# A decoder layer in fp32 on one core: the heads' scratch tiles of even and odd heads from one pool of fourteen slots instead of two of seven

## The chip, the core and the metric

The kernel runs on one core of a Trainium2 chip. The metric is the device time of one execution in microseconds, taken on the chip; lower is better. The core has a matrix engine (TensorE, PE in the profile), three engines for elementwise work (VectorE or DVE, ScalarE or ACT, GpSimd or POOL), and SyncE (SP), which in this kernel issues nearly all transfers between DRAM and the on-chip memory. Each engine runs its own instruction stream in order and waits on semaphores for the others.

## What is computed

One layer over 2048 tokens of width 1024, in fp32: a gated DeltaNet mixer with eight heads and a four-head attention over 256 memory rows, both read from one input projection; one output projection of the concatenated heads; a layer norm; a squared-ReLU MLP of width 4096; a layer norm.

```python
def gdn_mixer(x, mem_k, mem_v, w_in, conv_w, a_log, dt_bias, gate_norm_w, w_out):
    proj = x @ w_in                         # q, k, v, z, a, b, mq
    qkv = silu(causal_depthwise_conv(qkv, conv_w))
    q, k = l2_normalize(heads(q)), l2_normalize(heads(k))
    beta = sigmoid(b); g = -exp(a_log) * softplus(a + dt_bias)
    o = chunk_gated_delta_rule(q, k, v, g, beta)
    o = rms_norm(o, gate_norm_w) * silu(heads(z))
    m = memory_attention(mq, mem_k, mem_v)
    return concat([o, m]) @ w_out
...
x = layer_norm(ALPHA * x + mix)
x = layer_norm(ALPHA * x + square(relu(x @ w1)) @ w2)
```

In the delta rule each chunk of tokens inverts a unit lower triangular matrix (1 + beta k k^T with decay, below the diagonal) and then updates a state of 128 x 128 per head, chunk after chunk.

## The kernel before

**Blocks and stages.** The tokens go in four blocks of 512 (TB). For each pair of blocks (the loop over s at line 1752) come: the mixer of block 2s, the mixer of block 2s+1, the output projection of both (out_seven), the MLP's first product (ff1) and its second (ff2). A block's tokens are handled in chunks of 128, four at a time in one tile (NC). The projections and the MLP run as three fp32r products each (a high and a low part of both operands, mm3 at line 547). The output projection and the MLP use a scheme of seven products instead of eight for two blocks of tokens by two halves of the weights, so they keep sums of operands (S1 to S4, T1 to T4) in DRAM.

**The mixer.** The function mixer (line 1582) steps t from 0 to 9. In each step it records gdn_b for head t-2, then gdn_a for head t-1, then dense for head t, then a gate projection, memory heads and other work.
- dense(h) projects q, k and v, runs the convolution (ACT copies each PSUM bank to one of two raw tiles, DVE adds three taps from it), splits q and k into the tiles kq0 and kq1 (one buffer each), and writes kd, the transposed k with its decay (line 824).
- gdn_a(h) loads gb, a row of decays broadcast to all partitions (line 980), makes dl and at from it with a select on POOL and four exponentials on ACT each (lines 992 to 1003), multiplies both by the product pkq of k with k and q, two chunks at a time in one PSUM bank (lines 1005 to 1013), inverts dl (invert, line 851: an elimination loop of fifteen steps on DVE in the tiles Bc and Xc, then small matmuls through the single-buffered tiles of inv), keeps the inverse in Y, and makes vb and qd.
- gdn_b(h) runs the four chunks of the scan. It is a chain of PE, DVE, PE, ACT, PE, DVE per chunk and reads kd, at, Y, vb and qd to its end. The result goes to deliver (line 1203), which in the odd blocks also forms differences with the block before; for heads 6 and 7 it splits one of them into an "xh" and an "xl" tile at line 1230 for the product S2.

**The slots.** The function slot (line 463) asks for a tile of 128 x 512 fp32 from the pool sp under a tag; the number of slots of each tag is in BUFS (line 460). Seven tiles of a head (kd, gb, dl, at, Y, vb, qd) come from "s0" for even heads and from "s1" for odd heads, seven slots each. gb and dl are last read inside gdn_a, the other five by gdn_b. The same two tags serve later stages: in out_seven the tiles f (line 1679, "s0") and the low halves xl of operands S3, S4 and A22 as loaded from DRAM (line 1639: "s0" for n == 5, otherwise "s1"; six tiles for each of n = 3, 5 and 6); in ff1 operands kept through the stage (second_half, lines 1261 to 1263 and 1295); in ff2 the low halves of the last product (line 1470, alternating).

**The order of the work.** Nothing is issued while the functions above run. They only record operations (Recorder). At the end rec.issue (line 291) replays all of them with a duration for each, engine by engine: at every point the engine that can start first takes, among its operations that are ready, the one recorded first (rec.shift moves a few, rec.gate holds transfers back). A tile takes its slot when the first operation on it is otherwise ready. Slots of a tag are promised in the order in which the tiles are first used in the recording: a tile may take a free slot only if there are more free slots than tiles ahead of it that still have none. The lines that do this:

```python
if len(slots[b.key]) <= ahead(b):
    wait[b.key].append(o)
    return
b.held = True
b.since = heapq.heappop(slots[b.key])
```

The order found is the order in which the instructions stand in every engine's stream, so a changed number of slots can move any instruction behind the first tile that is touched by it. PSUM banks are tags of the same kind: "acc" with three banks for projections, "ga0" and "ga1" for gdn_a of even and odd heads, "pb" with two for gdn_b, "m".

Of the kernel before, what the change touches and what calls it, by code (L numbers as in the profile page):

```python
# [418 lines left out]
def hybrid_layer(  # L419
# [37 lines left out]
    dr = ctx.enter_context(tc.tile_pool(name="dr", bufs=2, space=bass.MemoryType.DRAM))  # L457

    NW, NR = 4, 3
    BUFS = {"d": 11, "th": 2, "s0": 7, "s1": 7, "on": 1, "iv": 4}  # L460
    PBUFS = {"acc": 3, "ga0": 1, "ga1": 1, "pb": 2, "m": 1}

    def slot(name, tag="s0", dt=F32, shape=(P, TB)):
# [331 lines left out]
    def dense(b, h, T, G, w0=None):  # L795
        res = {}
        for nm, o in (("q", QO), ("k", KO), ("v", VO)):
            w = w0 if w0 and nm == "q" else load_in(b, o // P + h)
            a = bank("a" + nm, "acc")
            project(a, w, T)  # L800
            c = slot("c" + nm, "d")
            th = slot("th", "th")
            if True:
                gi = o // P + h
                raw = rec.buf(tp, (P, TB + 3 + 56), F32, "raw", 2, "raw")
                nc.scalar.copy(out=raw[:, 3:TB + 3], in_=a)
                nc.gpsimd.tensor_copy(raw[:, 0:3], halo[:, gi].part(gi))
                if b < NB - 1:
                    nc.gpsimd.tensor_copy(halo[:, gi].part(gi), raw[:, TB:TB + 3])
                nc.scalar.activation(c, a, AF.Copy, scale=cw[:, 72 + gi:73 + gi])  # L810
                for j in range(3):
                    nc.vector.scalar_tensor_tensor(out=c, in0=raw[:, j:j + TB], scalar=cw[:, j * 24 + gi:j * 24 + gi + 1],
                                                   in1=c, op0=ALU.mult, op1=ALU.add)
                nc.scalar.activation(th, c, AF.Tanh, scale=0.5)
                nc.vector.scalar_tensor_tensor(out=c, in0=th, scalar=1.0, in1=c, op0=ALU.add, op1=ALU.mult)
            res[nm] = c
            if nm in "qk":
                if "kq" not in res:
                    res["kq"] = [rec.buf(tp, (P, 2, TB), F32R, "kq%d" % u, 1, "kq") for u in range(2)]
                i = "kq".index(nm)  # L820
                split(c, res["kq"][0][:, i].part(i), res["kq"][1][:, i].part(i), KQE)
        par = "ga%d" % (h % 2)
        ss = small("ss", [P, 2 * NC])
        kd = res["kd"] = slot("kd", "s%d" % (h % 2))
        for n, nm in enumerate("kq"):
            pt = bank("pt" + nm, par)
            for c in range(NC):
                nc.tensor.transpose(pt[:, c * P:(c + 1) * P], res[nm][:, c * P:(c + 1) * P], ident)
            for c in range(NC):
                j = small("j" + nm, [P, P], 1)  # L830
                nc.scalar.activation(j, pt[:, c * P:(c + 1) * P], AF.Square,
                                     accum_out=ss[:, n * NC + c:n * NC + c + 1])
            if nm == "k":
                for c in range(NC):
                    nc.scalar.activation(kd[:, c * P:(c + 1) * P], pt[:, c * P:(c + 1) * P], AF.Copy,
                                         scale=G["ekd"][:, h, c:c + 1])
        nc.gpsimd.tensor_scalar_add(ss, ss, 4 * RMS_EPS)
        rk = small("rk", [P, NC])
        nc.gpsimd.tensor_tensor(out=rk, in0=ss[:, :NC], in1=mhalf, op=ALU.pow)
        res["e4"] = small("e4", [P, NC], 4)  # L840
        nc.gpsimd.tensor_scalar_mul(res["e4"], ss[:, NC:], P * RMS_EPS)
        res["vbs"] = small("vbs", [P, NC])
        nc.gpsimd.tensor_tensor(out=res["vbs"], in0=G["betah"][:, h], in1=rk, op=ALU.mult)
        bh = res["bh"] = small("bh", [P, NC])
        nc.gpsimd.tensor_tensor(out=bh, in0=G["beta"][:, h], in1=rk, op=ALU.mult)
        nc.gpsimd.tensor_tensor(out=bh, in0=bh, in1=rk, op=ALU.mult)
        res["nbe"] = small("nbe", [P, NC], 4)
        nc.gpsimd.tensor_tensor(out=res["nbe"], in0=bh, in1=G["neg"][:, h], op=ALU.mult)
        return res

    def invert(L, par):
# [37 lines left out]
        ZT = small("ZT32", [P, NC, 32], 2)  # L889
        nc.vector.transpose(ZT.rearrange("p c f -> p (c f)"), Z.rearrange("p c f -> p (c f)"))  # L890
        XB, LB, X32, X64, Q = (inv[n] for n in ("XB", "LB", "X32", "X64", "Q"))
        Y = slot("Y", "s%d" % par)
        Y3 = v4(Y)
        nc.gpsimd.memset(Y, 0.0)
        quads = [slice(32 * q, 32 * q + 32) for q in range(4)]
# [79 lines left out]
    def gdn_a(h, r, G):  # L975
        par = h % 2
        q, k, v = (r[n] for n in "qkv")
        q3, k3, v3 = v4(q), v4(k), v4(v)
        sc = lambda n, c: G[n][:, h, c:c + 1]
        gb = slot("gb", "s%d" % par)  # L980
        nc.sync.dma_start(out=gb, in_=G["scr"][4 * h:4 * h + 4].rearrange("c i -> (c i)").partition_broadcast(P))
        gb3 = v4(gb)

        def trans(a3, nm):
            pt = bank(nm, "ga%d" % par)
            for c in range(NC):
                nc.tensor.transpose(pt[:, c * P:(c + 1) * P], a3[:, c], ident)
            return v4(pt)

        kd3 = v4(r["kd"])  # L990
        bh, vbs = r["bh"], r["vbs"]
        dl = slot("dl", "s%d" % par)
        dl3 = v4(dl)
        nc.gpsimd.affine_select(out=dl3, in_=gb3, compare_op=ALU.is_gt, fill=1e30,
                                base=0, pattern=[[0, NC], [-1, P]], channel_multiplier=1)
        for c in range(NC):
            nc.scalar.activation(dl3[:, c], dl3[:, c], AF.Exp, bias=sc("gc", c), scale=-1.0)
        at = slot("at", "s%d" % par)
        at3 = v4(at)
        nc.gpsimd.affine_select(out=at3, in_=gb3, compare_op=ALU.is_ge, fill=-1e30,  # L1000
                                base=0, pattern=[[0, NC], [1, P]], channel_multiplier=-1)
        for c in range(NC):
            nc.scalar.activation(at3[:, c], at3[:, c], AF.Exp, bias=sc("ngc", c))
        kh, kl = r["kq"]
        for c0 in range(0, NC, 2):
            pkq = bank("pkq", "ga%d" % par).rearrange("p (c u f) -> p c u f", c=2, u=2)
            for c in (c0, c0 + 1):
                cs = slice(c * P, (c + 1) * P)
                mm3(pkq[:, c - c0], kh[:, 0, cs], kl[:, 0, cs], kh[:, :, cs], kl[:, :, cs], True, True)
            for c in (c0, c0 + 1):  # L1010
                nc.vector.scalar_tensor_tensor(out=dl3[:, c], in0=pkq[:, c - c0, 0], scalar=bh[:, c:c + 1], in1=dl3[:, c],
                                               op0=ALU.mult, op1=ALU.mult)
            nc.vector.tensor_tensor(out=at3[:, c0:c0 + 2], in0=pkq[:, :, 1], in1=at3[:, c0:c0 + 2], op=ALU.mult)
        Y3 = invert(dl3, par)

        pv = trans(v3, "ptv")
        vb = slot("vb", "s%d" % par)
        vb3 = v4(vb)
        for c in range(NC):
            nc.scalar.activation(vb3[:, c], pv[:, c], AF.Copy, scale=vbs[:, c:c + 1])  # L1020
        qd = slot("qd", "s%d" % par)
        nc.scalar.activation(qd, gb, AF.Exp)
        nc.vector.tensor_tensor(out=qd, in0=qd, in1=q, op=ALU.mult)
        qd3 = v4(qd)

        return dict(k3=k3, kd3=kd3, vb3=vb3, at3=at3, qd3=qd3, Y3=Y3, nbe=r["nbe"], e4=r["e4"])
# [232 lines left out]
    def second_half(ys, T0d, B, between):  # L1259

        homes = {"T3": [slots("d", 4), slots("s0", 4)], "T2": [slots("d", 3), slots("s0", 3), halves("kq0", 1)],
                 "T4": [slots("s1", 3), slots("th", 2), slots("on", 1), halves("kq1", 1)],
                 "T1": [halves("tok", 4)], "B22": [slots("s1", 4), slots("iv", 4)]}
        homes = {n: [p for g in h for p in g] for n, h in homes.items()}
        for n, h in homes.items():
            B[n] = h[:4], h[4:]
# [25 lines left out]
                split(t3, B["T3"][0][k][:, c], B["T3"][1][k][:, c])  # L1292
        between()
        for k in K2:
            t4[k] = slot("b21", "s1")
            nc.sync.dma_start(out=t4[k], in_=T0d[:, 4 + k])
            t2 = wide("t2")
            sub(t2, e[k], t1[k])
            place("T2", k, t2)
            sub(t4[k], t4[k], t2)  # L1300
# [124 lines left out]
    def ff2(s, x1d):  # L1425
        ys = [tok_tile("y") for _ in range(2 * NC)]
        fresh = [[True, True] for _ in range(2 * NC)]
        gb = []
# [32 lines left out]
        def xpart(n, u, last):  # L1461
# [4 lines left out]
                return [(hi[:, j], lo[:, j]) for j in range(2)]  # L1466
            r = []
            for j in range(2):
                hi, lo = slot("xh", "d", F32R), slot("xl", "s%d" % j, F32R)
                split_in_place(hi, lo, xsc[n][:, 2 * u + j].part(2 * u + j))  # L1470
                r.append((hi, lo))
            return r
# [147 lines left out]
    def out_seven(s, x1d, T0d):  # L1620
# [10 lines left out]
        def operand(n, name, u):  # L1631
            if name == "S2" and u == 1:
                return [Xd[6], Xd[7]]
            if not XH[n][u]:
                x = []
                for j in range(2):
                    k = 2 * u + j
                    hi = slot("xh", "d" if n % 2 or k < 5 else "on", F32R)
                    lo = slot("xl", "s0" if n == 5 else "s1", F32R)
                    split_in_place(hi, lo, xo[name][:, k].part(k))  # L1640
                    x.append((hi, lo))
                return x
# [186 lines left out]
```

## Time and profile before

| | us |
|---|---|
| median of 3 runs | 2760.96 |
| lowest and highest | 2760.94, 2762.19 |
| the profiled execution, its own time | 2760.71 |
| its span, first to last instruction | 2759.0 |

The profile is of one execution. Its page gives each engine's busy time, a table in slices, the chain of work that ended last, and groups of instructions; further views list waits, the instructions of one tile, the order of time, and the busy time of each engine in chosen stretches. Since all operations are issued from one line of the program (402), tiles tell them apart. In a row such as "dl<-pkq,bh,dl" the written tile stands to the left. "[2.64 <-ACT whl]" behind a row means that the engine stood idle for 2.64 us before it and that an ACT instruction writing whl ended the wait, as far as the semaphores tell. PE is the matmul engine, PEld its weight loads, which overlap. PEclk is the granted clock of PE as a share of full speed. "x4" is the number of instructions put together in a row. In time the stages are: mixers of blocks 0 and 1 up to about 640, the first output projection up to about 790, the MLP up to about 1400, and the same again for blocks 2 and 3, with mixers to about 2010.

### The profile page before, as it was taken

What the parts mean: (1) busy time and instruction counts of PE and PEld (TensorE: products, weight loads), DVE (VectorE), ACT (ScalarE), POOL (GpSimd) and SP (SyncE); (2) the same over time, 40 slices, a digit from 0 to 9 for tenths busy, and PEclk for the clock granted to TensorE, in tenths of its full rate; (3) what the DMA queues carried; (4) which work ended last, traced back from release to release, by engine and by line L of the source; (5) the groups of instructions that cost most, each with busy time, mean ns of one, the idle gap of its engine ahead of it and who ended that gap; (6) DMA issues with size and microseconds to landing.
All of it is one profiled execution on the core that took longest, in us unless ns stands there. A gap on an engine that the chain in (4) does not pass through costs nothing.

```text
span 2759.0 us, 42405 instructions
## 1 busy us (share of the span) xinstructions
PE 2719.8 (99%) x13589; PEld 2267.0 (82%) x13589; DVE 2112.2 (77%) x5652; ACT 1642.3 (60%) x4082; POOL 403.7 (15%) x1030
## 2 busy tenths in 40 slices
PE   9999999999999999999999999999999999999998
PEld 7888888887788888888888888888887788888887
DVE  7889889998777777665778887888978665657575
ACT  7678767676485556334446676677855655544342
POOL 3233223321000000000023321223201000000000
PEclk9999999999999999999999999999999999999999
DMA  8565558876788888766754344444578744477673
GB/s 327 207 234 205 215 182 288 290 258 228 269 284 302 280 285 297 268 211 205 265 209 149 138 155 174 169 147 159 206 251 280 249 145 152 163 252 243 205 239 116
DMA packets 208543, 613.99 MB, mean 223 GB/s; under 512 B 23072, under 2 KB 32192, under 8 KB 188352
## 3 DMA queue, kind: packets, MB, share of 16 engines
q1 hardware_dynamic: 207888, 611.23, 63.5%
q8 instruction: 107, 1.75, 0.2%
q14 instruction: 116, 0.95, 0.1%
q10 hardware_dynamic: 432, 0.05, 0.0%
HBM read 436.54 MB, written 174.65 MB: 222 GB/s over the span
## 4 chain that ended last, share of the span: by engine, by line
PE 88%; ACT 7%; DVE 4%; issue 1%; POOL 1%; DMA 0%; DVEq 0%; SPq 0%; POOLq 0%; ACTq 0%
PE f2A L402 13%; PE fA L402 12%; PE ao L402 8%; PE f2C L402 6%; PE fC L402 6%; PE az L402 5%; PE aq L402 5%; PE av L402 5%; PE ak L402 5%; PE f2B L402 3%; PE fB L402 3%; PE amq L402 3%; PE pc L402 3%; PE po L402 2%; PE pkq L402 1%
## 5 line engine op out<-in xcount | busy, mean ns | idle before, releaser
L402 DVE TENSOR_TENSOR whl<-wraw,whl 128x512 fp32r<-128x512 f32 (+2 forms) x294 | 257.2, 884 | 109.4 <-ACT whl L402 107.0
L402 ACT CAST whl<-wraw 128x512 fp32r<-128x512 f32 (+2 forms) x294 | 226.5, 780 | 158.0 <-PE fC L402 52.0
L402 PE MATMUL fA<-B,whl 128*128 128x512 f32 x1152 | 277.2, 389 | 1.8 <-ACT B L402 1.5
L402 ACT CAST X<-X 128x1024 fp32r<-128x1024 f32 x118 | 123.9, 1052 | 236.2 <-DMA X<-xsc 196.2
L402 PE MATMUL f2A<-whl,X 128*128 128x512 f32 x1152 | 262.1, 389 | 0.0
L402 PEld LDWEIGHTS fA<-B,whl 128*128 128x128 f32 x1152 | 216.1, 188 | 47.5 <-ACT B L402 1.9
L402 PEld LDWEIGHTS f2A<-whl,X 128*128 128x128 f32 x1152 | 216.2, 188 | 44.9
L402 DVE TENSOR_TENSOR X<-X,X 128x1024 fp32r<-128x1024 f32 x118 | 144.2, 1223 | 129.0 <-ACT X L402 128.8
L402 PE MATMUL aq<-T,whl 128*128 128x512 f32 x768 | 214.3, 408 | 10.0 <-ACT T L402 5.5
L402 PE MATMUL az<-T,whl 128*128 128x512 f32 x768 | 213.0, 406 | 0.0
L402 PE MATMUL ak<-T,whl 128*128 128x512 f32 x768 | 211.4, 406 | 0.0
L402 PE MATMUL av<-T,whl 128*128 128x512 f32 x768 | 210.4, 404 | 0.0
L402 PE MATMUL fC<-B,whl 128*128 128x512 f32 x768 | 185.4, 389 | 0.3 <-DVE B L402 0.3
L402 PE MATMUL f2C<-whl,X 128*128 128x512 f32 x768 | 174.7, 389 | 0.0
L402 PEld LDWEIGHTS fC<-B,whl 128*128 128x128 f32 x768 | 144.1, 188 | 30.7 <-DVE B L402 0.8
L402 PEld LDWEIGHTS f2C<-whl,X 128*128 128x128 f32 x768 | 144.1, 188 | 29.9
L402 PEld LDWEIGHTS aq<-T,whl 128*128 128x128 f32 x768 | 136.5, 191 | 32.7 <-ACT T L402 5.5
L402 POOL TENSOR_SCALAR ve<-mv 128x1 f32<-128x1 f32 x34 | 16.4, 483 | 962.0 <-DVE mv L402 961.5
L402 PEld LDWEIGHTS av<-T,whl 128*128 128x128 f32 x768 | 137.3, 189 | 22.7
L402 PEld LDWEIGHTS ak<-T,whl 128*128 128x128 f32 x768 | 136.4, 189 | 23.5
L402 PEld LDWEIGHTS az<-T,whl 128*128 128x128 f32 x768 | 135.9, 189 | 21.6
L402 PE MATMUL ao<-whl,X 128*128 128x512 f32 x528 | 140.1, 404 | 3.5 <-DVE whl L402 1.3
(287 smaller groups left out, 6300.8 us busy)
## 6 DMA issues: line engine op xcount, KB each, us to landing
whl<-wsc SPq DMA_DIRECT2D x108, 1024.0 KB, 4.8
wraw<-in_w_ff_dram SPq DMA_DIRECT2D x106, 512.0 KB, 4.5
X<-xsc SPq DMA_DIRECT2D x96, 512.0 KB, 3.9
wsc<-whl SPq DMA_DIRECT2D x36, 1024.0 KB, 5.2
whl<-tsc SPq DMA_DIRECT2D x64, 512.0 KB, 4.7
xsc<-hB SPq DMA_DIRECT2D x96, 256.0 KB, 3.4
xo<-cat SPq DMA_DIRECT2D x80, 256.0 KB, 3.9
wraw<-in_w_in_dram SPq DMA_DIRECT2D x35, 512.0 KB, 5.9
```

The source lines that it names most:

```text
L402: o.fn(*[res(a) for a in o.args], **{k: res(v) for k, v in o.kw.items()})
```

## The change

The tag "s1" goes away and "s0" has fourteen slots. Every tile that came from "s1", or from "s0" or "s1" by the parity of its head, now comes from "s0". Memory, operations and their recorded order stay as they were.

```diff
-    BUFS = {"d": 11, "th": 2, "s0": 7, "s1": 7, "on": 1, "iv": 4}
+    BUFS = {"d": 11, "th": 2, "s0": 14, "on": 1, "iv": 4}
...
-        kd = res["kd"] = slot("kd", "s%d" % (h % 2))
+        kd = res["kd"] = slot("kd", "s0")
...
-        Y = slot("Y", "s%d" % par)
+        Y = slot("Y", "s0")
...
-        gb = slot("gb", "s%d" % par)
+        gb = slot("gb", "s0")
...
-        dl = slot("dl", "s%d" % par)
+        dl = slot("dl", "s0")
...
-        at = slot("at", "s%d" % par)
+        at = slot("at", "s0")
...
-        vb = slot("vb", "s%d" % par)
+        vb = slot("vb", "s0")
...
-        qd = slot("qd", "s%d" % par)
+        qd = slot("qd", "s0")
...
-                 "T4": [slots("s1", 3), slots("th", 2), slots("on", 1), halves("kq1", 1)],
-                 "T1": [halves("tok", 4)], "B22": [slots("s1", 4), slots("iv", 4)]}
+                 "T4": [slots("s0", 3), slots("th", 2), slots("on", 1), halves("kq1", 1)],
+                 "T1": [halves("tok", 4)], "B22": [slots("s0", 4), slots("iv", 4)]}
...
-            t4[k] = slot("b21", "s1")
+            t4[k] = slot("b21", "s0")
...
-                hi, lo = slot("xh", "d", F32R), slot("xl", "s%d" % j, F32R)
+                hi, lo = slot("xh", "d", F32R), slot("xl", "s0", F32R)
...
-                    lo = slot("xl", "s0" if n == 5 else "s1", F32R)
+                    lo = slot("xl", "s0" if n == 5 else "s0", F32R)
```

The PSUM banks "ga0" and "ga1" still go by the parity of the head.

## The prediction

> **What bounds the kernel now.** I read the page first, then the busy time of each engine by stage, then TensorE's waits and the order of time around them.
>
> ```profile
> span 2759.0 us, 42405 instructions
> PE 2719.8 (99%) x13589; PEld 2267.0 (82%) x13589; DVE 2112.2 (77%) x5652; ACT 1642.3 (60%) x4082; POOL 403.7 (15%) x1030
> PE 88%; ACT 7%; DVE 4%; issue 1%; POOL 1%; DMA 0%; DVEq 0%; SPq 0%; POOLq 0%; ACTq 0%
> ```
>
> TensorE (PE) is busy for all but 2759.0 - 2719.8 = 39.2 us, and the chain that ends last runs through it for 88%. The change adds and removes no arithmetic, so it can act only on those 39.2 us and on the clock. The table by stage says where they lie (columns: stretch, its length, then each engine's busy time; PEclk near the end).
>
> ```profile
> core 0: us, PE busy (x) PEld busy (x) DVE busy (x) ACT busy (x) POOL busy (x), PEclk, DMA share, GB/s
> 0.00:69.00 69.00, 62.82 (x288) 49.05 (x289) 53.15 (x108) 51.70 (x125) 25.79 (x64) 1.00 0.90 327
> 138.00:620.00 482.00, 479.07 (x2704) 404.43 (x2703) 430.98 (x1632) 358.73 (x1178) 144.18 (x362) 1.00 0.67 239
> 620.00:640.00 20.00, 17.27 (x98) 13.59 (x96) 18.14 (x72) 17.67 (x51) 6.66 (x13) 1.00 0.78 245
> 640.00:695.00 55.00, 54.17 (x298) 45.79 (x298) 47.45 (x160) 32.62 (x93) 6.77 (x18) 1.00 0.68 239
> 695.00:715.00 20.00, 16.52 (x79) 13.25 (x78) 10.55 (x18) 7.70 (x22) 1.46 (x3) 0.83 0.64 225
> 1448.00:2000.00 552.00, 548.47 (x3117) 465.78 (x3116) 460.93 (x1858) 385.54 (x1319) 144.31 (x412) 1.00 0.46 162
> 2000.00:2207.00 207.00, 203.86 (x980) 167.33 (x979) 155.05 (x311) 121.55 (x238) 11.23 (x26) 1.00 0.76 260
> 2690.00:2759.00 69.00, 59.77 (x264) 49.17 (x262) 39.95 (x54) 14.04 (x17) 6.29 (x8) 0.96 0.33 116
> ```
>
> The first and last slices hold 6.2 + 9.2 = 15.4 us that slots of the heads cannot reach. The mixers proper idle only 2.9 us (138 to 620) and 3.5 us (1448 to 2000). The end of block 1's mixer, 620 to 715, idles 2.7 + 0.8 + 3.5 = 7.0 us; the same place in block 3 lies within the 3.1 us of 2000 to 2207. One more stretch matters, because a gap there also cost clock:
>
> ```profile
> 82.00:84.50 2.50, 0.15 (x2) 0.00 (x0) 2.50 (x12) 1.62 (x4) 0.24 (x1) 1.00 0.00 0
> 84.50:91.30 6.80, 4.65 (x18) 3.97 (x19) 6.80 (x30) 0.35 (x1) 0.45 (x1) 0.50 0.30 93
> 702.00:705.70 3.70, 2.01 (x11) 1.34 (x10) 1.59 (x4) 1.84 (x6) 0.00 (x0) 1.00 0.52 167
> 705.70:712.50 6.80, 5.01 (x14) 3.86 (x15) 3.88 (x6) 4.36 (x13) 1.46 (x3) 0.50 0.48 163
> 2158.00:2166.00 8.00, 6.24 (x27) 4.60 (x26) 8.00 (x15) 5.97 (x12) 0.00 (x0) 1.00 0.92 335
> ```
>
> Twice the granted clock was 0.50 for 6.8 us, each time from inside a gap; 6.8 us at half rate are 3.4 us lost. The gap near 2160 (8.00 - 6.24 = 1.8 us) cost no clock. So the tail of block 1 loses 3.5 us idle and 3.4 us of clock within ten microseconds, and its cause is a slot:
>
> ```profile
> 702.64 0.39 PE L402 MATMUL po<-state,qd 128*128 128x128 f32 x2
> 703.06 1.93 SPq L402 DMA_DIRECT2D xl<-xo  x4
> 707.34 0.62 ACT L402 CAST xh<-xl 128x512 fp32r<-128x512 f32 x1
> 707.49 2.50 PE L402 MATMUL ao<-whl,xh 128*128 128x512 f32 x5 [2.64 <-ACT whl L402]
> ```
>
> The fourth product of the output projection (S3, line 1639) takes its xl tiles from "s1", which head 7 fills. Its last four loads are issued when the final read of head 7's qd ends (703.03), the first cast follows at 707.34, and PE stands for 2.64 us.
>
> **The change, part by part.** A head takes seven slots: kd, gb, dl, at, Y, vb, qd. gb and dl are given back inside gdn_a, the other five by gdn_b. With seven slots per parity, head h+2 gets kd and gb from head h's gb and dl, and everything else must wait for gdn_b of head h. That wait shows in the view of the tile dl and in the order of time for block 1's head 7:
>
> ```profile
> L402 ACT ACTIVATE dl<-dl,gc x128: 385/402/508, 65.1 to 1968.5; 128x128 f32<-128x128 f32 x128
> ...
> L402 POOL TENSOR_SCALAR_AFFINE_SELECT dl<-gb x32: 631/683/1097, 64.0 to 1966.7; 128x512 f32<-128x512 f32 x32
> ...
>   PE po L402: 39.5, 15
> ...
> 577.93 0.38 SPq L402 DMA_DIRECT2D gb<-scr  x1
> 601.67 0.63 ACT L402 ACTIVATE qd<-gb 128x512 f32<-128x512 f32 x1
> 610.37 0.22 DVE L402 COPY inv<-dl 64x128 f32<-64x128 f32 x1
> 622.25 0.76 PE L402 MATMUL pkq<-kq 128*128 128x256 f32 x5
> 624.44 0.39 PE L402 MATMUL po<-state,qd 128*128 128x128 f32 x2
> 624.91 0.68 POOL L402 TENSOR_SCALAR_AFFINE_SELECT dl<-gb 128x512 f32<-128x512 f32 x1 [0.57 <-PE po L402]
> 628.15 0.33 DVE L402 SCALAR_TENSOR_TENSOR dl<-pkq,bh,dl 128x128 f32<-128x128 f32 x1
> 631.84 0.41 DVE L402 TENSOR_TENSOR at<-pkq,at 128x256 f32<-128x256 f32 x1
> 632.31 0.98 PE L402 MATMUL pkq<-kq 128*128 128x256 f32 x6
> ```
>
> The input gb was fetched from 577.93 and the first pkq pair was done at 622.25 + 0.76 = 623.0. Yet dl began at 624.91, as head 5's last qd read (624.44 + 0.39) ended, the products at 628.15, and the second pair, waiting for the PSUM bank, at 632.31. In 15 of 32 heads POOL's idle time before dl ended on such a po.
>
> In one pool of fourteen the places are kept in order of first use: five for head h, five for head h+1 once its gb and dl are back, four for kd, gb, dl, at of head h+2. So dl and at no longer wait for gdn_b(h) but for gb and dl of head h+1. For head 7 those came back at 601.67 + 0.63 = 602.3 and 610.6, and then kq sets the pace: the products could follow the pair at 623.0 instead of at 628.15 and 631.84, 5.1 to 8.8 us sooner. I carry 6.
>
> What this moves: two selects of 0.68 us on POOL, which is 15% busy; eight exponentials on ACT, some 3.2 us at the 0.40 us of a row of this kind; on DVE the six products. All are as many as before. Behind the two selects POOL has the Y memset, which stays with gdn_b(h) and is read late. On SP the gb load falls back in the line: it was issued 47.0 us ahead of dl; it would now take the place that head 6's gb gives back at 602.3, still 22.6 us ahead of 624.91. Behind it on SP stand weight and X loads, issued in planned order. The cost is 0; uncovered it would be a load of this queue, 4.3 us by the xl rows above (703.06 to 707.34). kd of head h+3 now stands behind Y, vb, qd of head h+2, which take places at the same gdn_b end; cost 0.
>
> Two uses get worse places. In the odd blocks line 1230 asks for an xl for head 6's difference ahead of head 7's gb, so one of the fourteen is kept for it until its first write:
>
> ```profile
> L402 DVE TENSOR_TENSOR xl<-cat,xh x2: 685/687/689, 693.9 to 714.9; 128x512 fp32r<-128x512 f32 x2
> ```
>
> It is kept from 610 to 693.9, and head 7's at is the one that misses its place: it must still wait for head 5's gdn_b. And S3's six xl stand behind four f: 14 - 5 - 2 - 4 leaves 3 early loads against 2 now. The last three still wait for gdn_b(7).
>
> The sum. Head 6 is not touched by the kept place, so gdn_b(5) and (6) come 6 us sooner and at of head 7 with them. PE reaches S3 at about 702 either way; the loads need 4.3 us from the release, so a gdn_b(7) that ends 4.5 us sooner closes the gap. Terms: -3.5 us (702 to 707.5), -3.4 us (no half clock), -0.8 us of the 2.7 idle at 620 to 640, where ACT has both sets of exponentials and a memory softmax at once. Against that, the front of each inversion now competes for DVE (431.0 of 482.0 us busy): the 2.9 and 3.5 us of idle in the mixers grow; no row prices this. Bounds: they vanish (-6.4 us) or double (+6.4 us); I take +1.6, a quarter, since DVE's work is the same and only its order changes. Net -6.1 us: 2760.7 us, the profiled execution's own time (1.7 us outside the span), becomes 2754.6; the median shown is 2760.96, so I say 2755.
>
> The clock's price can be read in two ways. The row is 6.8 us at 0.50. The Trainium skill (TensorE: Matmul & The Clock Gate, "Why this matters for your kernels") asks for no idle gap above about 3 us, and gives a busy window of 3.4 us to come back. The trace disagrees with both: a 2.64 us gap went with the half clock and it lasted twice that. By 3.4 us at half rate the term would be -1.7 and the sum 2756.3.
>
> **The rivals.** (1) The tail stays. DVE, not the slot, sets head 7's chain, and the place kept for line 1230 eats the lead. For: DVE was busy 18.1 of 20.0 us at 620 to 640. Against: ACT and the slot, not DVE, delayed the products. Only the 0.8 us goes: 2760.
>
> (2) The change does not do what it says: Y, vb and qd of head h+1 are still without places when head h+2 asks, and the line is as long as two short ones. For: places are kept in order. Against: gb and dl of the head before are back 14 us before dl starts. 2761.
>
> (3) The gap closes but the half clock comes anyway, from the ragged stretch of 702 to 705.7 (2.0 of 3.7 us busy): -3.5 - 0.8 + 1.6, so 2758. The gate rows speak for it as far as 1.8 us near 2160 passed and 2.64 us here did not. The Trainium skill's 3 us (the same section) would have it so, since 2.64 us alone should not have tripped the clock.
>
> (4) Slower. Today head 7's elimination loop starts as head 6's ends; at the start of block 0 heads 0 and 1 ran theirs in step, and PE starved with DVE full.
>
> ```profile
> 82.44 0.25 DVE L402 TENSOR_TENSOR Bc<-Bc,Lc 128x24 f32<-128x24 f32 x2
> ...
> 641.02 0.22 DVE L402 TENSOR_TENSOR Xc<-Xc,Bc 128x60 f32<-128x60 f32 x1
> 641.15 0.16 DVE L402 TENSOR_TENSOR Bc<-Bc,Lc 128x4 f32<-128x4 f32 x1
> ```
>
> With dl sooner the loops overlap, the later head's steps go ahead of the next dense's taps (recorded later), raw's two tiles stay full, and the PSUM banks with them. The price is that of 82 to 91.3: 2.35 + 2.15 idle + 3.4 clock = 7.9 us, once, with the tail as it is: 2769. It decides where DVE has no slack for as long as the banks last. Against: DVE has a tenth of its time left in the mixers.
>
> **How the numbers follow.** A measurement of this kernel can tell about 0.2%, 5.5 us: below 2755.4 is faster, above 2766.5 slower. Chances: forecast 0.40 (faster), tail stays 0.22, no effect 0.08, half clock anyway 0.05 (all three the same), loops in step 0.25 (slower). Range: up to 2770 it takes in one starved stretch; down to 2746 it takes in the forecast with the mixers' idle gone too (2754.6 - 1.6 - 6.4 = 2746.6). The forecast's own range is 2746 to 2758.
>
> **What would show it.** Right: dl's select no longer ends its wait on po; PE without a gap before the S3 product near 700; PEclk 1.00 there. Wrong: the S3 loads still end on head 7's qd with a gap above 2 us behind; a new PEclk 0.50 in a mixer; or PE idle in 138 to 620 above 6 us with DVE near full.

## The result, and the profile after

The changed kernel takes 2766.07 us (median of 21 runs, 2762.53 to 2768.60), the kernel before, run beside it, 2761.63 us (21 runs, 2759.74 to 2764.41). The ratio is 1.0015 with a 95% interval of 1.0009 to 1.0022: slower by 0.15%, some 4.4 us, where 6 us less was forecast. It lies in the range on record and within what was called no change there, but the sign is the other one.

The profiled execution of the changed kernel took 2762.53 us and is the lowest of its runs, 3.5 us under their median; a second profile below shows what the others pay. First the page: the span, the busy times and the chain.

```profile
span 2760.8 us, 42380 instructions
PE 2722.8 (99%) x13589; PEld 2265.1 (82%) x13589; DVE 2117.8 (77%) x5652; ACT 1648.9 (60%) x4082; POOL 411.4 (15%) x1030
PE 83%; DVE 8%; ACT 5%; issue 2%; POOL 1%; DMA 1%; SPq 0%; DVEq 0%; POOLq 0%; ACTq 0%
```

TensorE is as full as before, yet the chain that ends last now runs 8% through DVE instead of 4%: more often it was DVE that released TensorE. Then busy time by stage, in the stretches used before, and two around a new place (columns as before):

```profile
138.00:620.00 482.00, 477.61 (x2690) 401.01 (x2689) 432.27 (x1632) 358.23 (x1179) 147.66 (x371) 1.00 0.68 239
620.00:640.00 20.00, 19.49 (x108) 16.37 (x107) 18.39 (x79) 16.69 (x44) 2.30 (x5) 1.00 0.61 195
640.00:695.00 55.00, 54.15 (x305) 45.53 (x305) 47.55 (x151) 33.34 (x94) 8.13 (x18) 1.00 0.70 246
695.00:715.00 20.00, 18.61 (x90) 14.86 (x89) 12.58 (x18) 9.57 (x22) 1.47 (x3) 1.00 0.95 352
1448.00:2000.00 552.00, 548.12 (x3113) 463.42 (x3112) 458.63 (x1837) 388.63 (x1313) 146.29 (x404) 1.00 0.46 160
2000.00:2207.00 207.00, 201.42 (x949) 164.19 (x948) 154.15 (x308) 120.94 (x235) 13.00 (x26) 0.99 0.75 258
...
2020.00:2026.00 6.00, 3.90 (x18) 2.89 (x16) 5.52 (x17) 1.04 (x1) 0.00 (x0) 1.00 1.01 319
2026.00:2036.00 10.00, 9.98 (x43) 8.24 (x44) 6.47 (x18) 4.71 (x15) 0.94 (x4) 0.83 0.38 127
```

Block 1's tail, 620 to 715, idles 0.5 + 0.9 + 1.4 = 2.8 us instead of 7.0, and the clock of 695 to 715 is whole. The mixers of blocks 0 and 1 idle 4.4 us instead of 2.9. Behind block 3's mixer 5.6 us are idle instead of 3.1, and the clock falls there.

Idle time is not all of it, since a product that starts a tenth of a microsecond late still counts as busy (a 128x512 product lasts 0.39 us, and the next start follows 0.23 us after its own). So I also lined the traces up by work: TensorE's products in the order of their starts, each weighted with the time of its shape, and the time at which a given sum of weights is reached. The weights only place the marks; the times are the trace's. Differences to before, by stretch:

```
us against before (its marks: 598.6, 716.1, 1441.3, 2011.0, end)
                       mixers 0,1  tail of 1  to block 2  mixers 2,3  rest   sum
changed, 1st profile       +6.6      -10.0       -1.7        +2.7     +4.3   +1.9
changed, 2nd profile       +7.1       -9.6       -1.8        +2.6     +6.8   +5.1
```

The gain that was forecast came at block 1's tail (-10.0 us by this count). It was eaten in three other places: the mixers of blocks 0 and 1, those of 2 and 3, and the stretch behind block 3's mixer. The second profile ran in 2765.97 us, close to the median of 2766.07, and differs mainly in the last. The split between the first two columns leans on the weights. With the median duration of a shape as its weight they come to +4.1 and -7.6, with the median distance between two starts to +5.4 and -8.9; their sum of -3.5 and the other columns hold within 0.4 us. The table by stage gives the tail without weights: 4.2 us less idle time and 3.4 us of clock, 7.6 us together.

The heads did what the slots allow. Rows of the tile dl over the whole run and of block 1's head 7 in the order of time, after:

```profile
L402 POOL TENSOR_SCALAR_AFFINE_SELECT dl<-gb x32: 635/642/2791, 64.0 to 1940.5; 128x512 f32<-128x512 f32 x32
its engine sat idle before it (us, times) until:
  PE pq L402: 97.4, 36
...
604.68 1.20 POOL L402 TENSOR_SCALAR_AFFINE_SELECT dl<-gb 128x512 f32<-128x512 f32 x1
619.72 0.65 POOL L402 TENSOR_SCALAR_AFFINE_SELECT at<-gb 128x512 f32<-128x512 f32 x1
...
619.74 0.34 DVE L402 SCALAR_TENSOR_TENSOR dl<-pkq,bh,dl 128x128 f32<-128x128 f32 x1
623.29 0.41 DVE L402 TENSOR_TENSOR at<-pkq,at 128x256 f32<-128x256 f32 x1
...
625.08 0.39 PE L402 MATMUL po<-vt,at 128*128 128x128 f32 x2
...
696.46 0.39 PE L402 MATMUL po<-state,qd 128*128 128x128 f32 x2
```

The wait on po has gone. dl comes 20.2 us sooner (604.68, was 624.91), the products 8.4 us (619.74, was 628.15) and the last read of qd 6.2 us (696.46, was 702.64). The row at 625.08 is head 5's last read of its own at.

The new place is behind block 3's mixer: SyncE's queue, ACT and TensorE after, then the clock of the second profile.

```profile
2018.04 0.40 SPq L402 DMA_DIRECT2D xo<-cat  x1
2018.49 0.42 SPq L402 DMA_DIRECT2D cat<-xo  x1
2019.01 0.45 SPq L402 DMA_DIRECT2D X<-xo  x1
...
2024.92 1.04 ACT L402 CAST X<-X 128x1024 fp32r<-128x1024 f32 x1 [5.84 <-DMA X<-xo]
...
2026.02 5.30 PE L402 MATMUL ao<-whl,X 128*128 128x512 f32 x15 [2.12 <-ACT X L402]
```
```profile
2020.00:2024.80 4.80, 4.78 (x22) 3.61 (x20) 4.80 (x13) 0.00 (x0) 0.00 (x0) 1.00 0.94 261
2024.80:2028.20 3.40, 0.04 (x1) 0.05 (x1) 1.66 (x9) 1.05 (x1) 0.00 (x0) 0.90 0.99 377
2028.20:2035.00 6.80, 6.80 (x20) 5.40 (x20) 3.85 (x9) 1.91 (x5) 0.00 (x0) 0.55 0.39 125
```

An operand X is fetched behind the stores and loads of the heads' differences (cat and xo); TensorE stands 2.12 us and then has 3.4 us of half clock. The same fetch in before:

```profile
2020.77 0.41 SPq L402 DMA_DIRECT2D X<-xo  x1
...
2024.93 1.05 ACT L402 CAST X<-X 128x1024 fp32r<-128x1024 f32 x1 [3.10 <-DMA X<-xo]
```

So X is not later than in before: it is asked for 1.8 us sooner, takes 5.9 instead of 4.2 us until ACT casts it (from 2020 to 2024.8 the DMA share is 1.02, in before 0.76), and is cast at the same time. TensorE, by work 2.4 us ahead of before here, has nothing else ready. In the second profile X is asked for 0.9 us later than in the first and cast 2.1 us later; TensorE stands 3.4 us and has 6.8 us of half clock: 1.3 + 1.7 = 3.0 us more, most of the 3.4 us between the two runs.

### The profile page after: what moved, and what is told of

The parts are those of the page before. It is cut to its first block, busy times and chain, and to the rows that moved or that the text cites. A ratio compares the mean times of both kernels' runs of the same rounds, so it can differ in the third digit from the quotient of the medians.

```text
span 2760.8 us, 42380 instructions
## 1 busy us (share of the span) xinstructions
PE 2722.8 (99%) x13589; PEld 2265.1 (82%) x13589; DVE 2117.8 (77%) x5652; ACT 1648.9 (60%) x4082; POOL 411.4 (15%) x1030
## 4 chain that ended last, share of the span: by engine, by line
PE 83%; DVE 8%; ACT 5%; issue 2%; POOL 1%; DMA 1%; SPq 0%; DVEq 0%; POOLq 0%; ACTq 0%
PE f2A L402 13%; PE fA L402 12%; PE f2C L402 6%; PE ao L402 6%; PE fC L402 6%; PE aq L402 5%; PE ak L402 5%; PE az L402 4%; PE av L402 4%; PE f2B L402 3%; PE fB L402 3%; PE amq L402 3%; PE pc L402 3%; PE po L402 2%; PE pkq L402 1%
```

## The experiments

Theory 1: a head's early front (dl and at) is paid for in the mixers. Theory 2: any new order draws small stalls anew, and before's is a lucky one. Theory 3: the loss at the end comes from the later users (f, xl, b21), which now stand in the heads' line.

**Memory, heads and later users apart.** In four kernels all tiles lie in one pool of fourteen, but the planner keeps two groups of seven, and only tiles with the tag "sm" may take a place of either group (the counting loop is shortened here).

```diff
+        pools = {"s0": [0.0] * 7, "s1": [0.0] * 7}
+            c = ...  # tiles ahead that still have no place, by tag
+            if b.tag == "sm":
+                ok = len(pools["s0"]) + len(pools["s1"]) > sum(c.values())
+                return min(((pools[g][0], g) for g in pools if len(pools[g]) > c[g]), default=(0, None))[1] if ok else None
+            return b.tag if len(pools[b.tag]) > c[b.tag] + c["sm"] else None
...
+    def head_tag(h):
+        return "sm" if (at_block[0], h) in MERGED else "s%d" % (h % 2)
```

> One pool of fourteen in memory, but the planner goes on promising places as in two groups of seven (six kinds of tile, seven places per parity). The order of the instructions on every engine is that of before; only addresses and some semaphores differ. If the slowdown comes from the order alone (all theories but one): the time of before, within 3 us. If it comes from where the tiles lie in memory: slower by about 4.5 us, as the change is.

> The seven tiles of the heads go through one pool of fourteen, the later users (f, xl, b21, the kept operands of the MLP) stay in groups of seven. Theory 1, the heads' earlier front costs in the mixers: mixers of blocks 0 and 1 +5.5 us, of blocks 2 and 3 +3.7 us, tail of block 1 about -10 us, all as in the changed kernel. Theory 3, the loss behind block 3's mixer (+3.4 to +4.7 us) comes from the later users' new line: that loss is gone, so about -1 us against before. If it too comes from the heads: +3 to +5 us against before.

> The heads stay in two groups of seven and only the later users take any of the fourteen. Theory 1: the mixers are those of before; block 1's tail keeps its gap and half clock or loses part of it, since the loads of the fourth product of the output projection can take places of either group: 0 to -5 us. Theory 3: the loss of 3.4 to 4.7 us behind block 3's mixer appears here. Theory 2, that every new order draws new small stalls of a few us with either sign: anywhere from -6 to +6 us, in stages that this edit does not touch too.

> Only heads 5 to 7 of block 1 take any of the fourteen; all other heads and the later users stay in their groups. The order up to head 5 of block 1 is that of before. Theory 1: the mixers keep before's stalls and the tail of block 1 gains as in the changed kernel, so -8 to -11 us against before, 2751 to 2753 us. Theory 2: the gain of the tail comes, and the stages behind it, whose order is drawn anew, move by several us with either sign: -16 to -2 us.

Measured, medians against 2762.60 us for before: memory only 2760.59, heads only 2759.83, later users only 2776.36, last heads only 2754.91 (ratio 0.9972, 0.9962 to 0.9983). By work:

```
                       mixers 0,1  tail of 1  to block 2  mixers 2,3  rest   sum
memory only                -0.8       +1.0       +0.5        -0.8     +1.4   +1.3
heads only                 +8.1      -10.1       +0.0        +2.7     +0.1   +0.8
later users only           -0.1      +16.6       +2.8        -0.8     -1.5  +17.0
last heads only            +2.1       -6.6       -0.5        -1.1     -0.1   -6.2
```

Memory costs nothing. The heads alone bring both the gain at the tail and the price in the mixers, as theory 1 has it. The loss at the end needs the later users as well: with the heads alone it is gone. But the later users alone do not bring it, so theory 3 is only half right; they lose at block 1's tail instead, 17.0 us in all where 6 at most was forecast. By the rule above, the xl of line 1230 asks ahead of head 7's gb and keeps a free place of gb's group from it (read from the rule; no row shows a kept place). What follows from it is in the rows of the tile gb and of the products that read qd.

```profile
L432 SPq DMA_DIRECT2D gb<-scr x1: 422/422/422, 622.1 to 622.1; - x1
  DMA gb<-scr: 4.7, 1
...
L432 PE MATMUL po<-state,qd x24: 272/275/422, 606.0 to 722.2; 128*128 128x128 f32 x24
```

gb is fetched at 622.1 instead of 577.9, now uncovered, and head 7's scan ends near 722 instead of 703.

With heads 5 to 7 of block 1 alone the mixers of blocks 2 and 3 stay as they were and TensorE meets the fourth product without a gap (order of time, TensorE):

```profile
700.72 0.73 PE L432 MATMUL ao<-whl,X 128*128 128x512 f32 x2
701.29 0.43 PE L432 MATMUL pc<-vt,kd 128*128 128x128 f32 x2
701.55 0.39 PE L432 MATMUL po<-vt,at 128*128 128x128 f32 x2
701.70 5.26 PE L432 MATMUL ao<-whl,X 128*128 128x512 f32 x22
706.80 0.49 PE L432 MATMUL pto<-ident,on 128*128 128x128 f32 x3
```

It beats both kernels: 7.7 us under before in the same runs, just short of the 8 to 11 forecast, as three heads already cost 2.1 us in block 1's mixer and gain 6.6 instead of 10 at its tail. It is one order, the same as before's up to head 5 of block 1, and it was not redrawn. The profile of the kernel with the heads alone was its slowest run (2761.91 us), so its sum of +0.8 stands 2 us above its median.

**Redraws.** The planner's safety time, MARGIN, is changed by a few nanoseconds in both kernels. No term of the argument depends on it, but in the traces some four in ten places of the engines' streams (38 to 44%) hold another instruction than in the first order of the same kernel, more than the forecast below names.

```diff
-MARGIN = 100
+MARGIN = 97
```

> The kernel before with the planner's safety time MARGIN 97 ns instead of 100. Nothing is meant by it: some 3000 to 3800 places in the engines' streams hold another instruction. Theory 1, before's pools give calm mixers whatever the draw: mixers of all four blocks within 2 us of before in sum, total 2760 to 2765. Theory 2, before's order is a lucky draw: its mixers lose 4 to 10 us as the changed kernel's do.

> As the run with 97, with 103 ns. Theory 1: within 2 us of before in the mixers, 2760 to 2765 in all. Theory 2: another draw, mixers 4 to 10 us dearer.

> The changed kernel with MARGIN 97 ns. Theory 1: the mixers of blocks 0 and 1 again cost about 5.5 us and those of 2 and 3 about 3.7 us more than before's, and block 1's tail again gains about 10 us; the 3 to 5 us lost behind block 3's mixer come again if they belong to the one line for the later users, and are gone if they were one load's bad luck: 2758 to 2767. Theory 2: the mixers' cost falls anywhere between 0 and 10 us, so 2752 to 2768.

> As the changed kernel with 97, with 103 ns: by theory 1 mixers some 9 us dearer than before's again, by theory 2 anywhere between 0 and 10; the gain in block 1's tail, which no theory disputes, comes in both.

> The kernel before with a planner margin of 95 ns. If its first order is a lucky draw, as two redraws say (2771.4 and 2770.6): 2766 to 2774. If those two were the unlucky ones: 2760 to 2765. The stretch from block 2's first projection to its output projection stays at 586 to 589 us in either case.

> The changed kernel with a margin of 95 ns. Lucky first draw: within 5 us of before with the same margin, either sign. Lasting loss: 4 to 8 us above it. The stretch of blocks 2 and 3 at 591 to 595 us by both.

> The kernel before with a planner margin of 105 ns. Lucky first draw: 2766 to 2776, as with 95, 97 and 103 (2774.1, 2771.4, 2770.6). If those three were the unlucky ones: 2760 to 2765.

> The changed kernel with a margin of 105 ns: 2764 to 2775, within 7 us of before with the same margin, either sign. In the stages, as in its other draws: the mixers 5 to 12 us above before's first draw, block 1's tail 9 to 11 us below it.

```
margin                 95       97      100      103      105     mean
before            2774.08  2771.38  2761.63  2770.58  2770.22  2769.58
changed           2767.07  2774.09  2766.07  2768.50  2776.24  2770.39
difference           -7.0     +2.7     +4.4     -2.1     +6.0     +0.8

mean of five profiles, against before's own
                       mixers 0,1  tail of 1  to block 2  mixers 2,3  rest
before                     +4.8       -0.5       +3.8        -0.1     +0.8
changed                    +6.8       -9.3       +4.9        +2.9     +4.5
mixers 2,3, each: before +0.7 -1.5 0.0 +0.1 +0.4; changed +4.2 +2.3 +2.7 +3.1 +2.2
```

Theory 2 holds for the total. Before at margin 100 is 8.6 to 12.5 us better than each of its own redraws; the five differences have a mean of +0.8 us with a standard error of 2.4, so a lasting loss is not shown, nor a gain. Before's good draw lies in the mixers of blocks 0 and 1 (its four redraws lose 6.0 us there on average) and, which no theory had, in the stretch to block 2 (4.8 us). Several forecasts were missed: before with 97 and 103 came some 6 us above theory 1's range, the change with 97 came 6 us above the wider of its ranges, with 95 it was 7.0 us under before, which neither reading had, and with 105 it came 1.2 us above its range and its tail gained 4 to 5 us instead of 9 to 11. Theory 1 holds for two stages, where no draw of one kernel reaches a draw of the other: the mixers of blocks 2 and 3 (3.0 us dearer) and block 1's tail up to its mark (8.8 us cheaper). With median durations as weights these are 2.7 and 6.8 us, and still no draw reaches the other side, though the tails come as close as -3.3 and -3.9. In the mixers of blocks 0 and 1 the draws overlap: of the 6.6 us that the pair compared shows, 2.0 us are left on average (0.2 by the other weights), and the rest is before's good draw.

The mark at 716 hides something. The half clock that the change removed from the first output projection comes back in each of its redraws, from 729 us on (in one of them half of it at 708.7). Busy time by stage, the change in its first order, then with margin 97:

```profile
700.00:760.00 60.00, 58.36 (x260) 47.08 (x259) 52.01 (x78) 27.98 (x46) 4.26 (x8) 1.00 0.74 267
```
```profile
700.00:760.00 60.00, 55.25 (x245) 44.36 (x243) 44.36 (x67) 21.53 (x39) 1.81 (x3) 0.94 0.65 233
```

PEclk is 0.94 there in before and in all eight redraws, that is 6.8 us of half clock, and 1.00 in the first order of the change alone. TensorE idles 5.2 us there in before, 1.6 in the change and 4.6 to 5.7 in its redraws (3.8 to 5.6 in before's). What the redraws of the change keep lies ahead of it: from 620 to 700 they idle 0.0 to 1.2 us at full clock, before and its redraws idle 3.0 to 4.2 us, and before's redraws add 3.4 or 6.8 us of half clock near 640.

**The front held back.** In the changed kernel the planner makes dl's select wait again for gdn_b of the head two before.

```diff
+        if self.hold is not None:
+            preds[self.hold.i] = self.hold
...
+        rec.hold = scans.get(h - 2) if True else None
         nc.gpsimd.affine_select(out=dl3, in_=gb3, compare_op=ALU.is_gt, fill=1e30,
...
+            scans[h] = rec.ops[-1]
```

In the second of the two kernels `True` becomes `at_block[0] != 1`, so that block 1 goes unheld.

> The changed kernel, but in the planner each head's dl select also waits for the last product of gdn_b of the head two before, as the two pools made it wait; everything else stays in one pool of fourteen. Measured so far, from the first projection of block 2 to its output projection: 588.3, 586.5 and 586.6 us in three orders of before, 593.6, 592.1 and 592.0 us in three orders of the changed kernel. Theory 1, the early front of a head (dl and at) is what the mixers pay for: that stretch comes back to 586 to 589 us, and block 1's tail loses its gain (the first output projection and its gap as in before): 2760 to 2770 in all. Theory 1b, the cost comes from the other merged tiles or the later users: it stays at 592 to 594.

> As the run with the front held, but block 1's heads are let go early. Theory 1: the stretch of blocks 2 and 3 at 586 to 589 us, and the last reads of block 1's head 7 near 700 instead of 705, so no gap ahead of the fourth product: some 8 us less than with all fronts held. Theory 1b: 592 to 594 us in blocks 2 and 3.

```
                       mixers 0,1  tail of 1  to block 2  mixers 2,3  rest   sum
front held                 +0.1       -4.2       +4.2        +0.8     +0.7   +1.6
held but in block 1       +10.5      -10.8       +3.6        +0.8     +0.1   +4.2
```

Medians 2764.51 and 2766.55 us (before 2762.84). The stretch named in the forecast runs from the first product of the tile aq in block 2 to the first of ao, here in before and after the change:

```profile
L402 PE MATMUL aq<-T,whl x384: 387/393/483, 1405.5 to 1942.7; 128*128 128x512 f32 x192
...
L402 PE MATMUL ao<-whl,X x264: 387/390/499, 1993.8 to 2097.0; 128*128 128x512 f32 x132
```
```profile
L402 PE MATMUL aq<-T,whl x384: 387/393/482, 1400.3 to 1942.2; 128*128 128x512 f32 x192
...
L402 PE MATMUL ao<-whl,X x264: 387/390/628, 1993.9 to 2100.0; 128*128 128x512 f32 x132
```

That is 588.3 and 593.6 us; over all five draws it is 585.4 to 589.6 in before and 590.8 to 593.9 in the change. With the front held it is 589.8 and 589.7 us. By work the mixers are back: +0.1 and +0.8 instead of +6.6 and +2.7. In blocks 0 and 1, where before's own draws spread over 6 us, this says little; in blocks 2 and 3 it says that the early front is what they pay for, and of the front the early dl, since at was not held (in block 1 head 6's at was made at 578.3, in before at 595.9). The loss behind block 3's mixer is gone too (+0.7 and +0.1), although the later users stay in the one pool: in these orders it takes both. The stretch came out 1 us longer than forecast, just above before's draws and below the change's, and the 8 us between the two kernels did not appear, because block 1's mixer lost them: unheld, it had a starved stretch (its order of time, then its clock).

```profile
530.65 0.60 PE L404 MATMUL pp<-inv 128*128 128x32 f32 x4 [0.23 <-ACT inv L404]
534.09 0.63 PE L404 MATMUL pq<-YP,inv 128*128 128x64 f32 x4 [2.84 <-DVE YP L404]
535.57 1.09 PE L404 MATMUL pp<-inv 128*128 128x64 f32 x4 [0.85 <-ACT inv L404]
...
531.00:534.60 3.60, 0.76 (x7) 0.66 (x6) 3.39 (x12) 3.45 (x10) 0.00 (x0) 1.00 0.98 294
534.60:541.60 7.00, 5.53 (x18) 4.47 (x17) 6.84 (x21) 4.67 (x16) 1.18 (x3) 0.54 0.98 353
```

TensorE waits 2.84 us inside an inversion while DVE is busy 3.39 and ACT 3.45 of 3.60 us, and the half clock follows: a starved stretch, as in the prediction's rival of the slower side, in another kernel than the changed one. It is not two elimination loops in step, since DVE's rows from 526 to 534 hold splits of weights (wk) and small copies of the inversion and no step of a loop; whether letting block 1 go or the draw made it isn't shown. In the kernel with all fronts held the gap did not stay ahead of the fourth product as forecast (0.23 us there), it moved to the next one (2.45 us at 731.9, waiting for a weight).

**The last head alone.** As with heads 5 to 7, for head 7 only.

> Only head 7 of block 1 takes any of the fourteen places; its dl and at come early, all else as in before. Theory 1: the gain of block 1's tail with the least of the mixers' cost: 2 us better than with heads 5 to 7, so 2752 to 2754, if head 7's own front is what closed the gap; 2758 to 2762 if heads 5 and 6 had to come sooner too, as the chain of scans in order would have it.

2759.05 us against 2762.84 (ratio 0.9991, 0.9982 to 1.0000). Its dl came at 610.6, but the second pair of products still at 632 and the last read of qd at 704.8, no sooner than before, with the half clock behind. The profile is of its slowest run (2762.87 us), so most runs lost less than it shows. Heads 5 and 6 have to come sooner too: the scans run in order, and one early front has nothing to run into.

**The change once more.**

> The changed kernel once more, for a second profile: its first profiled execution (2762.53 us) was the lowest of 21 runs, their median 3.5 us above it. A step of that size should stand at one place: a half clock of 3.4 or 6.8 us in a stage where the first profile has none. If instead the 3.5 us are spread over all stages, the span grows evenly.

The step stood at one place, as shown with the result: 2.5 us of the 3.2 us between the two profiles lie behind block 3's mixer.

**DVE made lighter.** Two of three convolution taps are left out in both kernels, so q, k and v are others; 6 x 0.747 us less on DVE for each head.

```diff
-                for j in range(3):
+                for j in range(2, 3):
```

> The kernel before without two of the three convolution taps of each projection (this changes what is computed): 6 of 0.747 us less on DVE for each head, some 4.5 us of about 54. Only the stretch of blocks 2 and 3 is read here: 584 to 588 us, since TensorE bounds it.

> The changed kernel without two of the three taps (this changes what is computed). If the early front costs because it competes for DVE, the stretch of blocks 2 and 3 comes within 2 us of before without them (it was 5.4 us longer with all taps). If the cost lies in the order of TensorE's own stream, it stays 4 to 6 us longer.

Busy time by stage, first before, then the change, both without the two taps:

```profile
138.00:620.00 482.00, 479.23 (x2713) 404.90 (x2712) 404.70 (x1604) 359.35 (x1182) 142.94 (x371) 1.00 0.69 242
1448.00:1980.00 532.00, 528.86 (x3030) 450.61 (x3029) 401.31 (x1707) 377.46 (x1302) 137.01 (x404) 1.00 0.46 159
```
```profile
138.00:620.00 482.00, 479.75 (x2721) 405.91 (x2720) 403.97 (x1606) 359.10 (x1182) 140.83 (x373) 1.00 0.69 244
1448.00:1980.00 532.00, 529.45 (x3032) 449.89 (x3031) 399.96 (x1694) 374.88 (x1290) 131.86 (x398) 1.00 0.45 159
```

With DVE at 404 instead of 432 us of 482 the change idles TensorE less than before does (2.2 against 2.8 us, then 2.6 against 3.1). By work its mixers cost the same: -2.6 against -2.2 us in blocks 0 and 1, -0.8 against -1.0 in 2 and 3. The stretch of blocks 2 and 3 is 592.9 against 591.9 us, within the 2 us of the forecast, but mostly because before's grew by 3.6 us: it missed its own forecast of 584 to 588, since where that stretch ends also depends on how much of the scans is done by then. The count by work is the better witness: there before gained 1.0 us and the change 3.5 against their first orders with all taps (0.0 and +2.7). In a single run each, the lightened change takes 2745.27 us and the lightened kernel before 2750.73. So the early front's price hangs on DVE's load: with less of it none was seen. That is a pointer, not a proof. It is one draw of each, and in blocks 0 and 1, where draws differ by 4 us and more, that alone would show little; in blocks 2 and 3 no two draws of one kernel differ by more than 2.2 us, and the 3.0 us are gone.

## Why the prediction had the wrong sign, point by point

**The slots: right.** dl and at no longer wait for gdn_b of head h-2. Head 7's products were forecast 5.1 to 8.8 us sooner, 6 carried: the products came 8.4 us and the end of the scan 6.2 us sooner. gb fell back to 595.3 (forecast 602.3) and cost nothing. That head 7's at would have to wait for head 5's gdn_b was wrong: its select ran at 619.72, and head 5 read its own at until 625.08 + 0.39. The prediction has gdn_b of heads 5 and 6 come 6 us sooner; the last reads of their qd came 1.9 us (622.5, was 624.4) and 3.0 us (669.9, was 672.9) sooner, and only head 7's own 6.2. The run with head 7 alone shows that the heads ahead of it had to come sooner for the gain, as the text had it. Three of the six xl of the fourth product are fetched early instead of two, as forecast.

**The tail of block 1: right in size for the pair compared, in part by luck, and its cause misread.** Forecast -3.5 - 3.4 - 0.8 = -7.7 us; measured -7.6 by idle time and clock, -10.0 by work, and -8.8 by work on average over five draws up to the mark at 716. But the half clock and most of the gap that the forecast counts, -3.5 - 3.4, went away in the first order alone; in all four redraws of the change they stand in the same output projection. And the slot of xl, which the prediction calls the cause of the gap, is not what its row names: the wait ended on ACT's cast of whl.

```profile
706.41 1.03 ACT L402 CAST whl<-whl 128x1024 fp32r<-128x1024 f32 x1
```

It ended at 707.44, TensorE went on at 707.49, and the first cast of a late xl ended only at 707.96. ACT had been held by head 7's scan (its last copy of vt at 703.83) and squared head 7's result between the two casts of whl. In the kernel with head 7 alone three xl were fetched early, as in the change, and the gap was 2.64 us again, ended by whl; with the front held the scan ended no sooner than in before, whl's second cast came at 705.75, and 0.23 us were left. So the place of whl's casts in ACT's stream closes or opens this gap; that the xl loads alone would have held it is not shown.

**The mixers: the step that failed.** "Bounds: they vanish (-6.4 us) or double (+6.4 us); I take +1.6, a quarter, since DVE's work is the same and only its order changes." The mechanism named there, competition for DVE, is the one that the lightened runs point to, but the term was mis-sized: +6.6 + 2.7 = +9.3 us in the pair compared (+6.5 with median durations as weights), beyond the bound of 6.4, and +2.0 + 3.0 = +5.0 us over draws (+2.9), where +1.6 was taken. Two reasons. The bound was made from idle time alone, and idle time of 138 to 620 grew by only 1.5 us, to 4.4, so that the sign given for it (above 6 us) did not show; the rest are starts that come late without the table counting them as idle. And 4.3 us of the 9.3 are no cost of the change but the good order of before, which its redraws do not have.

**Behind block 3's mixer: left out.** "The same place in block 3 lies within the 3.1 us of 2000 to 2207", and it had no term. It has no gap to win, but a new one to lose: +4.3 us in the first profile and +6.8 in the second, +3.7 on average over the draws. It appears with heads and later users together and with neither alone, and not with dl held back; one draw of before lost 4.2 us there too. What in the line slows the fetch of X was not tried, so its cause stays open beyond the rows shown.

**The sum.** Forecast -7.7 + 1.6 = -6.1. In the first profile -10.0 - 1.7 + 6.6 + 2.7 + 4.3 = +1.9, and with the typical end +5.1. Over draws -8.8 + 1.1 + 2.0 + 3.0 + 3.7 = +1.0, which agrees with the +0.8 of the medians.

**The rivals.** That the change does nothing is refuted by the 20.2 us of dl. That the tail stays is refuted by the 7.6 us of the pair compared, but in the redraws the gap and the half clock of the output projection do stay. That the half clock comes anyway was wrong in the pair compared; in the redraws of the change it came, behind gaps of its own and not from the ragged stretch that the rival names. The slower side came, but not as loops in step that starve TensorE once: the changed kernel has no new starved stretch in a mixer. The loss is spread over small stalls: from 138 to 620 TensorE waits 12 times for more than 0.15 us, where before has 7 such waits and its redraws 9 to 13. A starved stretch is seen in the kernel held but in block 1, without two loops in step.

## What to carry to other kernels

Before a change of order is priced, redraw the order of the kernel before: here a neutral nudge of 3 to 5 ns cost 8.6 to 12.5 us, more than the change, and a good order is a lucky one until shown otherwise. An earlier start is worth something only where the end waits for it; elsewhere it can spend the slack of the fullest helper engine (here DVE, 432 of 482 us). Letting go just the last heads took 7.7 us off here, in one order that was not redrawn. Read what a wait ended on before a cause is named: the gap called the slot's ended on a cast of weights. Bound a loss by lost time against work done, not by the idle time of a view.

## What the hardware showed that was not expected

Half clock came in pieces of 3.41, 6.83 or 10.24 us in the profiles here (the last ten microseconds of the span aside; the changed kernel without two taps has no other). How long a gap must be for it isn't fixed. The same product behind the same gap of 1.49 us, in before and in the kernel with one pool in memory only, whose order is the same (order of time, TensorE, then the clock of the two):

```profile
2162.93 0.49 PE L402 MATMUL fA<-B,whl 128*128 128x512 f32 x1 [1.49 <-ACT B L402]
...
2160.00:2170.00 10.00, 8.24 (x36) 6.25 (x35) 9.67 (x17) 7.30 (x15) 0.00 (x0) 1.00 0.64 233
```
```profile
2162.46 0.50 PE L432 MATMUL fA<-B,whl 128*128 128x512 f32 x1 [1.49 <-ACT B L432]
...
2162.50:2165.90 3.40, 3.14 (x8) 2.29 (x9) 3.40 (x7) 3.09 (x7) 0.00 (x0) 0.68 0.84 348
2165.90:2170.00 4.10, 4.10 (x17) 3.29 (x16) 3.38 (x6) 1.84 (x5) 0.00 (x0) 0.85 0.04 16
```

Before kept the whole clock; the other ran at half clock for one piece of 3.41 us that lies across the two stretches, so it lost (1 - 0.68) x 3.4 + (1 - 0.85) x 4.1 = 1.7 us. Elsewhere 2.12 us of idle time brought 3.4 us of half clock, 2.64 brought 6.8, and 3.1 (before with margin 97) only 3.4. The Trainium skill (TensorE: Matmul & The Clock Gate, "Why this matters for your kernels") warns of idle gaps above about 3 us. The rows differ from it: half the length was enough once, and a longer gap cost less than a shorter one. Why, no run here shows.
